# A transformer block on one core: pooling mixer issued before the third head, a serial inverse without raised priority, and four smaller moves

## The chip, the cores and the metric

The kernel runs on one core of a Trainium2 chip. Its engines are TensorE (PE in the profile, with its weight loads as PEld), VectorE (DVE), ScalarE (ACT), GpSimd (POOL) and SyncE (SP, which here only issues transfers). The metric is the device time of one execution in microseconds; the median of three runs is given. The profile comes from one more execution, taken by the hardware profiler.

## The reference

One block of a model on 1024 tokens of width 1024 (f32), cut to what matters here:

```python
h = rms_norm(x, attn_norm)
xa, qkv, z, b, a, c_q, c_kv, k_pe = split(h @ w_in)
y_a = pool_mixer(xa)              # windows 2, 4, 8, 16: (csum - shifted csum)/count - xa, then a 64x64 product per group
y_b = gated_deltanet(qkv, z, b, a)  # conv of 4 taps, silu, 4 heads of 128, chunks: triangular solve, then a serial scan
y_c = mla_attention(c_q, c_kv, k_pe)  # 4 heads, causal softmax
x = x + concat(y_a, y_b, y_c) @ w_out
x = x + square(relu(rms_norm(x) @ w_up)) @ w_down
```

The delta-rule part needs, for each head and chunk, the inverse of a unit triangular matrix and then a scan over chunks in which each step needs the state of the step before.

## The kernel before, in words

**Precision and projections.** Every large product is made of three f32r matmuls on high and low parts (`mm3`, L122): hi·hi, hi·lo, lo·hi. The input projection is cut into 18 column tiles of 128. `proj_tile` (L479) computes one tile in two halves of 512 tokens; a half is 8 x 3 = 24 matmuls of 128x512 into one of four PSUM banks tagged "mm". The tiles run in `tile_order` (L472): 6 to 9 are keys, 14 to 17 gates, 2 to 5 queries, 10 to 13 values, 0 and 1 the input of the pooling mixer. `prefetch` loads the next tile's weights and splits them: ACT casts the high part, and the low part is a subtraction on GpSimd, or on VectorE for the tiles 15, 2 and 10. Two tiles of split weights fit at a time.

**What a half brings.** A query, key or value half is evicted by `conv_silu` (L495): one ACT copy, three scalar-tensor-tensor instructions on VectorE (L502), a tanh on ACT and one product (L510). A value half is then transposed by four TensorE transposes (L697, inside `values`) right after it. A gate half is one ACT and one VectorE instruction (L710). A half of the mixer's input is one ACT copy (L653).

**Side work.** Generators give small steps to be put between halves: after each half `proj_tile` calls `pump(n, m)`, which takes n steps of the queue `side` and m of `slow`. `side` holds first `lanes()` (L576), then `heads(0, 1)`, then `heads(2, 3)`. `lanes()` inverts 128 triangular 32x32 blocks, one per partition, in 31 serial steps of two VectorE instructions (L586, L588), written to memory at its end. In before these stand under `tc.high_priority(offset=3000)`. `heads` runs `levels` (small fp32 products at L751 that build the inverse of 128x128 blocks) and then `chain`, the scan of 8 chunks, for two heads in turn: 76 steps for a pair. 8 steps a half are pumped at the first two gates, SIDE = 10 at queries and values, LATE = 12 at the last gates and mixers.

**Order.** Keys; gates 0, 1; then query and value of heads 0 to 3, with `heads(0, 1)` appended after head 1 and `heads(2, 3)` after head 3; gates 2, 3; first halves of both mixers. Then eight `load_k` (L886 to L893) turn the attention keys; the first mixer's second half stands at the first of them. The attention loop (L1029 on) takes the second mixer's second half in its first group and then `pool` (shifted sums on GpSimd, L612 to L631) and `pool_out`, step by step. `load_v` (L901) splits the attention values on GpSimd. `while slow` pumps `pool(0)` after the key loads.

**After attention.** `out_tile` (L1107) makes 8 x 2 half tiles of x + mixed·w_out. `square` (L1120) squares each on ACT, and GpSimd adds the square into `acc` (L1128); `stats` (L1135) sums over partitions by TensorE from `acc` and the last square; between the second halves the first up-projection weights are split and summed, `s_2` on GpSimd. The MLP follows, in a Strassen-like form.

The instructions are traced in this order, and a planner with a cost model of its own fixes each engine's order at compile time, by order of issue among what it believes ready. On the chip each engine then runs its list in that order.

Of the kernel before, what the change touches and what calls it, by code (L numbers as in the profile page):

```python
# [16 lines left out]
ALU = mybir.AluOpType  # L17
AX = mybir.AxisListType

P = 128  # L20
# [17 lines left out]
YU = 20  # L38
LAG = 2
OFF = 2  # L40
SIDE = 10
LATE = 12
BANKS = {"mm": 4, "sm": 2, "ch": 2, "s2": 2}
WINDOWS = (2, 4, 8, 16)
QK = 96
# [18 lines left out]
def block_kernel(ctx, tc, x, x_t, params, positions, attn_norm, w_tiles, w_g, w_qb, w_kvb, w_out,  # L64
                 w_up, w_down, out, dbg=None):
    nc = tc.nc
# [37 lines left out]
    def MM(tag="mm"):  # L104
        pool, w = (wide[0], 512) if tag == "mm" else (wide[0], 1024) if tag == "s2" else (ps, 512)
        return pool.tile([P, w], F32, tag=tag, name=nm(tag), bufs=BANKS[tag])
# [338 lines left out]
    def load_w(src, shape=(P, KD, P), eng=None):  # L445
        raw = S(shape, "raw", 3)
        nc.sync.dma_start(raw, src)
        hi, lo = S(shape, "w", 4, F32R), S(shape, "w", 4, F32R)
        split(hi, lo, raw, eng)
        return hi, lo  # L450

    side, slow, ahead = [], [], []

    def step(queue, n):
        for _ in range(n):
# [7 lines left out]
    def pump(n, m=0, a=AH):  # L463
        step(slow, m)
        step(ahead, a)
        step(side, n)

    def drain():
        while slow or side or ahead:
            pump(1, 1, 1)  # L470

    tile_order = [6, 7, 8, 9, 14, 15, 2, 10, 3, 11, 4, 12, 5, 13, 16, 17, 0, 1]  # L472
    loaded = {}

    def prefetch(ct):
        if ct not in loaded:
            loaded[ct] = load_w(w_tiles[ct], eng=V if ct in (15, 2, 10) else G)

    def proj_tile(ct, use, n=0, m=1, halves=(0, 1), tag="mm", between=None):  # L479
        prefetch(ct)  # L480
        hi, lo = loaded[ct]
        nxt = tile_order.index(ct) + 1
        for hf in halves:
            if hf == halves[-1] and nxt < len(tile_order):
                prefetch(tile_order[nxt])
            pm = MM(tag)
            for k in range(KD):
                mm3(pm, hi[:, k, :], lo[:, k, :], ht_hi[hf][:, k, :], ht_lo[hf][:, k, :], k == 0, k == KD - 1)
            use(hf, pm)
            pump(n, m)  # L490
            if between and hf == halves[0]:
                between()
# [83 lines left out]
    def lanes():  # L576
        TL = U((P, 32, 32), s="tl")
        TLT = U((P, 32, 32), s="tlt")
        G.memset(TL.rearrange("p a b -> p (a b)"), 0.0)
        G.affine_select(out=TL, in_=TL, compare_op=ALU.not_equal, fill=1.0, base=0, pattern=[[1, 32], [-1, 32]], channel_multiplier=0)  # L580
        tmp = U(s="lt")
        for j in range(31):
            n, m = 31 - j, j + 1
            tv = tmp[:, 512 * (j % 2):512 * (j % 2) + n * m].rearrange("p (a b) -> p a b", a=n)
            with tc.high_priority(offset=3000):
                V.tensor_tensor(tv, L[:, j, j + 1:32].unsqueeze(2).to_broadcast([P, n, m]),  # L586
                                TL[:, j, 0:m].unsqueeze(1).to_broadcast([P, n, m]), op=ALU.mult)
                V.tensor_tensor(TL[:, j + 1:32, 0:m], TL[:, j + 1:32, 0:m], tv, op=ALU.subtract)  # L588
            yield
        with tc.high_priority(offset=3000):  # L590
            V.tensor_copy(TLT, TL.rearrange("p a b -> p b a"))
            nc.sync.dma_start(t_dram[0], TL.rearrange("p a b -> p (a b)"))
            nc.scalar.dma_start(t_dram[1], TLT.rearrange("p a b -> p (a b)"))
        yield

    side.append(lanes())
# [68 lines left out]
    def v4(ap):  # L665
        return ap.rearrange("p (a b) -> p a b", a=4)

    def queries(h):
        qt = QT[h] = U(s="qt")
        proj_tile(2 + h, conv_silu(h, qt), SIDE)  # L670

    def query_key(h):
        qt = QT[h]
# [12 lines left out]
    def values(h):  # L686
        vs = VS[h] = U((P, NC, P), s="vs")
        vt = [None, None]

        def half(hf):  # L690
            vt[hf] = W()
            return vt[hf]

        def use_v(hf):
            pt = MM("sm")
            for j in range(4):
                PE.transpose(pt[:, j * P:(j + 1) * P], vt[hf][:, j * P:(j + 1) * P], ident)  # L697
            for j in range(4):
                c = 4 * hf + j
                A.activation(vs[:, c, :], pt[:, j * P:(j + 1) * P], AF.Copy, scale=sk[:, h, c:c + 1])  # L700

        return 10 + h, conv_silu(8 + h, half, use_v)

    def gate(h):
        zs = ZS[h] = U(s="zs")

        def use_z(hf, pm):
            th = W()
            A.activation(th, pm, AF.Tanh, scale=0.5)
            V.scalar_tensor_tensor(zs[:, hf * 512:(hf + 1) * 512], th, 1.0, pm, op0=ALU.add, op1=ALU.mult)  # L710

        return 14 + h, use_z
# [129 lines left out]
    def heads(*hs):  # L842
        for stage in (levels, chain):
            gens = [stage(h) for h in hs]
            while gens:
                for g in list(gens):
                    try:
                        next(g)
                        yield
                    except StopIteration:  # L850
                        gens.remove(g)
# [1 line left out]
    dn_half = const((P, 1), "dn_half")  # L853
    V.tensor_scalar(dn_half, pv("dn_norm"), 0.5, None, op0=ALU.mult)
    for h in range(2):
        proj_tile(*gate(h), 8, 2)
    for h in range(H):
        queries(h)
        proj_tile(*values(h), SIDE, between=lambda: query_key(h))
        if h % 2:  # L860
            side.append(heads(h - 1, h))
    for h in (2, 3):
        proj_tile(*gate(h), LATE)
    mix = [mixer(i) for i in range(2)]
    for i in range(2):
        proj_tile(*mix[i], LATE, halves=(0,))


    k_hi, k_lo = (S((QK, H, 1024), "H", 4, F32R) for _ in range(2))
# [134 lines left out]
    begin = [[m for m, _ in pairs].index(m) for m in ms_]  # L1004
    turn_at = {max(begin[k] - 1, begin[k - 1]): k for k in range(1, 4)}
    for t in range(NT):
        if t == 0:
            proj_tile(*mix[0], LATE, halves=(1,))
            slow.append(pool(0, XA[0]))
        load_k(t)  # L1010
        pump(2, 1)
        if t == 1:
            load_q(ms_[0])
            turn_q(ms_[0])
            load_q(ms_[1])
    while slow:
        pump(0, 1)
    mid.close()
    wide[0] = mid.enter_context(tc.tile_pool(name="pa", bufs=2, space=PSUM))
    prs = [U(s="pr"), U(s="pr")] + [None] * 4  # L1020

    def mixer_end():
        proj_tile(*mix[1], 0, 0, halves=(1,), tag="sm")
        slow.extend((pool(1, XA[1]), pool_out(0), pool_out(1)))
        yield

    prev = [None] * OFF
    wo_raw = None
    for n in range(len(pairs) + OFF):  # L1029
        if n in turn_at:  # L1030
            turn_q(ms_[turn_at[n]])
            if turn_at[n] < 3:
                load_q(ms_[turn_at[n] + 1])
        if n == 1:
            v_hl = S((P, NT, 2, 4, 64), "H", 4, F32R)
            HB = S((P, 4, 1024), "H", 4)
            prs[2:6] = [HB[:, q, :] for q in range(4)]
            for t in range(NT):
                load_v(t)
        gens, cur = [], None  # L1040
        if n < len(pairs):
            m, hs = pairs[n]
            prp = [prs[(2 * n) % 6], prs[(2 * n + 1) % 6]]
            steps = [1024 // len(hs) if i > 1 else (i + 1) * P for i in (2 * m, 2 * m + 1)]
            gens = [scores(i, hs, prp[i % 2], V if n < 2 else G) for i in (2 * m, 2 * m + 1)]
            if n == 0:
                gens.append(mixer_end())
            cur = (m, hs, prp, steps)
        todo = []
        old = prev.pop(0)  # L1050
        if old:
            pm_, phs, pprp, psteps = old
            todo = [(pm_, hh, j, g, pprp, psteps) for g, hh in enumerate(phs) for j in range(0, 2 * pm_ + 2, 2)]
        while gens or todo:
            if gens:
                try:
                    next(gens[0])
                except StopIteration:
                    gens.pop(0)
                    continue  # L1060
            if todo:
                piece(*todo.pop(0))
                weigh(2)
            step(side, 2)
            if n > 0:
                step(slow, 1)
            if n == len(pairs) and wo_raw is None:
                wo_raw = wo_load(0, "w", 4)
                wo = [S((P, 2, 8, 256), "H", 4, F32R)]
                late = wo_split(wo[0], wo_raw)  # L1070
            if n >= len(pairs):
                next(late, None)
        prev.append(cur)
        while side and n == 1:
            step(side, 1)
# [45 lines left out]
    def square(k, hf, n):  # L1121
        hs = slice(512 * hf, 512 * hf + 512)
        if n == 0:
            return A.activation(acc[:, hs], x2[k][:, hs], AF.Square)
        sq = HM(s="sq")
        ins = A.activation(sq, x2[k][:, hs], AF.Square)
        if n < KD - 1:
            G.tensor_tensor(acc[:, hs], acc[:, hs], sq, op=ALU.add)  # L1128
        else:
            sq_last[0] = sq  # L1130
        return ins
# [416 lines left out]
```

## Time and profile before

| what | value |
|---|---|
| median of 3 runs | 1245.23 us (1244.7 to 1245.61) |
| profiled execution | 1246.01 us |
| its span, first to last instruction | 1243.5 us |
| PE busy | 1173.8 us (94%) |
| DVE busy | 864.1 us (69%) |
| ACT busy | 571.3 us |
| POOL busy | 292.2 us |
| mean granted clock of TensorE | 0.968 |

The span is what the instructions cover; the rest of an execution's time lies around it. A busy PE is not yet a PE at full speed: the granted clock tells which of its two levels (1.2 or 2.4 GHz) it had.

### The profile page before, as it was taken

The numbers are of one execution on the slowest core, as the hardware profiler recorded it, in microseconds if no ns is written. First come the engines' busy times: TensorE is split into PE (matmuls) and PEld (weight loads), VectorE is DVE, ScalarE is ACT, GpSimd is POOL, SyncE is SP. The second block draws the span as 40 slices with busy tenths as digits, with TensorE's granted clock in tenths as the row PEclk, the third lists the DMA queues.
The fourth block names the chain that finished last, engine by engine and source line by source line (L and its number), as shares of the span: only waits on it lengthen the run. The fifth ranks groups of instructions, "written<-read, shape, count | busy, mean of one in ns | idle before, by whom it ended". The sixth has DMA issues, their size and how long they took to land.

```text
span 1243.5 us, 16293 instructions
## 1 busy us (share of the span) xinstructions
PE 1173.8 (94%) x5802; PEld 970.4 (78%) x5802; DVE 864.1 (69%) x1551; ACT 571.3 (46%) x1187; POOL 292.2 (23%) x323
## 2 busy tenths in 40 slices
PE   6999997899999769999799999999999999999998
PEld 5967776788887658788587788888888888888887
DVE  7576659838726758735788776676659897786863
ACT  6554531544534458622346454555554433333330
POOL 0135541011200266422505434243220000000000
PEclk9999999889989779999889999999999999999999
DMA  6102331121120130191314434434469964443202
GB/s 255 65 21 72 132 102 52 60 43 40 30 53 7 62 119 2 62 345 62 108 54 150 176 138 167 154 144 161 148 227 339 375 219 155 152 136 102 94 27 100
DMA packets 85697, 152.60 MB, mean 123 GB/s; under 512 B 25456, under 2 KB 28656, under 8 KB 85616
## 3 DMA queue, kind: packets, MB, share of 16 engines
q1 hardware_dynamic: 76624, 144.23, 32.9%
q10 hardware_dynamic: 8992, 7.34, 1.9%
q8 instruction: 45, 0.74, 0.2%
q14 instruction: 36, 0.29, 0.1%
HBM read 105.41 MB, written 46.14 MB: 122 GB/s over the span
## 4 chain that ended last, share of the span: by engine, by line
PE 74%; DVE 15%; ACT 4%; POOL 4%; issue 2%; DMA 1%; SPq 0%; DVEq 0%; ACTq 0%; POOLq 0%
PE mm L1423 14%; PE mm L1179 13%; PE sm L1179 6%; PE ch L1423 5%; PE sm L1423 5%; PE mm L125 4%; PE mm L123 4%; PE mm L124 4%; PE ch L1179 3%; PE sm L751 2%; DVE t2k L502 2%; DVE H L116 1%; PE ch L125 1%; DVE tl L588 1%; PE ch L123 1%
## 5 line engine op out<-in xcount | busy, mean ns | idle before, releaser
L1423 PE MATMUL mm<-dop,dop 128*128 128x512 f32 x768 | 176.0, 389 | 0.0
L1423 PEld LDWEIGHTS mm<-dop,dop 128*128 128x128 f32 x768 | 144.1, 188 | 29.9
L1179 PE MATMUL mm<-H,wop 128*128 128x512 f32 x576 | 140.2, 396 | 3.8 <-DVE uo L1247 3.8
L1179 PEld LDWEIGHTS mm<-H,wop 128*128 128x128 f32 x576 | 109.4, 191 | 28.2 <-DVE uo L1247 5.1
L115 ACT CAST dop<-wdr 128x1024 fp32r<-128x1024 f32 x48 | 50.4, 1050 | 151.6 <-PE mm L1423 62.9
L123 PE MATMUL mm<-H,w 128*128 128x512 f32 x280 | 115.3, 412 | 2.7 <-DVE zs L710 2.7
L124 PE MATMUL mm<-H,w 128*128 128x512 f32 x280 | 115.0, 411 | 0.0
L125 PE MATMUL mm<-H,w 128*128 128x512 f32 x280 | 114.9, 410 | 0.0
L1179 PE MATMUL sm<-op,wop 128*128 128x512 f32 x384 | 92.2, 389 | 0.0
L116 POOL TENSOR_TENSOR w<-raw,w 128x1024 fp32r<-128x1024 f32 x15 | 36.6, 2438 | 206.2 <-ACT w L115 142.4
L1179 PEld LDWEIGHTS sm<-op,wop 128*128 128x128 f32 x384 | 72.1, 188 | 15.0
L116 DVE TENSOR_TENSOR dop<-wdr,dop 128x1024 fp32r<-128x1024 f32 x48 | 58.6, 1221 | 31.0 <-ACT dop L115 31.0
L1269 ACT ACTIVATE uo<-uo 128x512 f32<-128x512 f32 x48 | 30.3, 631 | 99.4 <-DVE uo L1247 59.2
L1423 PE MATMUL sm<-dop,dop 128*128 128x512 f32 x288 | 67.4, 389 | 0.0
L1423 PE MATMUL ch<-dop,dop 128*128 128x512 f32 x288 | 67.4, 389 | 0.0
L116 DVE TENSOR_TENSOR wop<-s,wop 128x512 fp32r<-128x512 f32 x64 | 47.1, 751 | 26.1 <-ACT wop L115 26.1
L502 DVE SCALAR_TENSOR_TENSOR t2k<-mm,cw,t2k 128x511 f32<-128x511 f32 (+2 forms) x72 | 53.5, 743 | 14.2 <-ACT t2k L499 9.4
L116 DVE TENSOR_TENSOR dop<-H,dop 128x1024 fp32r<-128x1024 f32 x52 | 63.2, 1216 | 0.0
L123 PEld LDWEIGHTS mm<-H,w 128*128 128x128 f32 x280 | 54.0, 193 | 11.6 <-DVE zs L710 3.1
L1423 PEld LDWEIGHTS sm<-dop,dop 128*128 128x128 f32 x288 | 54.1, 188 | 11.2
L1423 PEld LDWEIGHTS ch<-dop,dop 128*128 128x128 f32 x288 | 54.0, 188 | 11.2
L125 PEld LDWEIGHTS mm<-H,w 128*128 128x128 f32 x280 | 54.1, 193 | 8.9
(397 smaller groups left out, 2659.9 us busy)
## 6 DMA issues: line engine op xcount, KB each, us to landing
H<-u_dram SPq DMA_DIRECT2D x52, 512.0 KB, 4.5
upr<-in_w_up_dram SPq DMA_DIRECT2D x38, 512.0 KB, 4.0
u_dram<-t SPq DMA_DIRECT2D x64, 256.0 KB, 2.0
wdr<-in_w_down_dram SPq DMA_DIRECT2D x32, 512.0 KB, 8.1
u_dram<-uo SPq DMA_DIRECT2D x48, 256.0 KB, 2.0
raw<-in_w_tiles_dram SPq DMA_DIRECT2D x18, 512.0 KB, 3.3
wor<-in_w_out_dram SPq DMA_DIRECT2D x10, 512.0 KB, 8.6
x<-in_x_dram SPq DMA_DIRECT2D x8, 512.0 KB, 3.6
```

Of the source, the lines that this page charges most:

```text
L115: A.copy(hi, src)
L116: (eng or V).tensor_tensor(lo, src, f32(hi), op=ALU.subtract)
L123: PE.matmul(o, ah, bh, start=first, stop=False)
L124: PE.matmul(o, ah, bl, start=False, stop=False)
L125: PE.matmul(o, al, bh, start=False, stop=last)
L502: V.scalar_tensor_tensor(acc[:, s:], pm[:, :512 - s], w, acc[:, s:], op0=ALU.mult, op1=ALU.add)
L588: V.tensor_tensor(TL[:, j + 1:32, 0:m], TL[:, j + 1:32, 0:m], tv, op=ALU.subtract)
L751: PE.matmul(pa[:, c, :], lhs[:, c, :], rhs[:, c, :], start=True, stop=True)
L1179: PE.matmul(o, x_, y_, start=(first and j == 0 and q == 0), stop=(j == 3 and q == 2), skip_group_check=True)
L1269: A.activation(o, o, AF.Relu)
L1423: PE.matmul(o, x_[:, cs_], y_, start=(q in (0, 1, 3) and i == 0 and e == 0), stop=(i == GP - 1 and e == 2), skip_group_check=True)
```

## The change

The mixers (tiles 0 and 1) move from the end of the projections to the place between head 1 and head 2 (tiles 4, 12, 5 and 13 come after them), where `heads(0, 1)` starts; `pool(0)` and `pool(1)` are queued right there. The second halves of the gates 2 and 3 take the place that the mixers' halves had beside the key loads. `lanes()` loses its raised priority and is pumped 4 steps a half over gates 0, 1 and head 0. `SIDE` is 7 and `LATE` is gone. The transposes of a value half wait in a list `later` until the next half has been evicted. Weights of tiles 3 and 11 are split on VectorE too. The sums of squares are added on VectorE.

```diff
-SIDE = 10
-LATE = 12
+SIDE = 7
+LANE = 4
...
-    tile_order = [6, 7, 8, 9, 14, 15, 2, 10, 3, 11, 4, 12, 5, 13, 16, 17, 0, 1]
+    tile_order = [6, 7, 8, 9, 14, 15, 2, 10, 3, 11, 0, 1, 4, 12, 5, 13, 16, 17]
...
-            loaded[ct] = load_w(w_tiles[ct], eng=V if ct in (15, 2, 10) else G)
+            loaded[ct] = load_w(w_tiles[ct], eng=V if ct in (15, 2, 10, 3, 11) else G)
...
             pm = MM(tag)
+            due = later[:]
+            del later[:]
             for k in range(KD):
                 mm3(...)
             use(hf, pm)
+            for f in due:
+                f()
             pump(n, m)
...
-            with tc.high_priority(offset=3000):
-                V.tensor_tensor(tv, ...)
-                V.tensor_tensor(TL[:, j + 1:32, 0:m], ...)
+            V.tensor_tensor(tv, ...)
+            V.tensor_tensor(TL[:, j + 1:32, 0:m], ...)
...
         def use_v(hf):
+            later.append(lambda: turn_v(hf))
+
+        def turn_v(hf):
             pt = MM("sm")
...
     for h in range(2):
-        proj_tile(*gate(h), 8, 2)
+        proj_tile(*gate(h), LANE, 2)
     for h in range(H):
-        queries(h)
-        proj_tile(*values(h), SIDE, between=lambda: query_key(h))
-        if h % 2:
-            side.append(heads(h - 1, h))
-    for h in (2, 3):
-        proj_tile(*gate(h), LATE)
-    mix = [mixer(i) for i in range(2)]
-    for i in range(2):
-        proj_tile(*mix[i], LATE, halves=(0,))
+        n = LANE if h < 2 else SIDE
+        queries(h, n)
+        proj_tile(*values(h), n, between=lambda: query_key(h))
+        if h == 1:
+            drain()
+            side.append(heads(0, 1))
+            for i in range(2):
+                proj_tile(*mixer(i), SIDE, 3)
+                slow.append(pool(i, XA[i]))
+    side.append(heads(2, 3))
+    ends = [gate(h) for h in (2, 3)]
+    for z in ends:
+        proj_tile(*z, SIDE, halves=(0,))
...
     for t in range(NT):
-        if t == 0:
-            proj_tile(*mix[0], LATE, halves=(1,))
-            slow.append(pool(0, XA[0]))
         load_k(t)
         pump(2, 1)
         if t == 1:
+            proj_tile(*ends[0], SIDE, halves=(1,))
+        if t == 3:
             load_q(ms_[0])
             turn_q(ms_[0])
             load_q(ms_[1])
+        if t == 5:
+            proj_tile(*ends[1], SIDE, halves=(1,))
...
-    def mixer_end():
-        proj_tile(*mix[1], 0, 0, halves=(1,), tag="sm")
-        slow.extend((pool(1, XA[1]), pool_out(0), pool_out(1)))
-        yield
+    slow.append(pool_out(0))
+    slow.append(pool_out(1))
...
-            if n == 0:
-                gens.append(mixer_end())
...
-            G.tensor_tensor(acc[:, hs], acc[:, hs], sq, op=ALU.add)
+            V.tensor_tensor(acc[:, hs], acc[:, hs], sq, op=ALU.add)
```

## Rows read from the trace of the kernel before

**Rows 1.** The page's head: the span.

```profile
span 1243.5 us, 16293 instructions
```

**Rows 2.** Stretches: time, busy (instructions) of PE, PEld, DVE, ACT, POOL; clock; DMA; GB/s.

```profile
170.00:210.00 40.00, 39.75 (x168) 32.62 (x168) 30.52 (x63) 6.17 (x8) 17.04 (x25) 0.96 0.27 88
210.00:221.00 11.00, 0.23 (x2) 0.02 (x1) 10.05 (x28) 1.23 (x2) 0.00 (x0) 0.73 0.29 120
221.00:256.00 35.00, 33.72 (x178) 28.02 (x179) 26.24 (x60) 20.99 (x66) 8.86 (x8) 0.94 0.22 51
346.00:407.00 61.00, 60.77 (x435) 50.50 (x434) 30.06 (x113) 26.68 (x85) 4.99 (x4) 0.92 0.09 27
407.00:450.00 43.00, 25.90 (x124) 20.80 (x124) 26.57 (x52) 18.15 (x43) 23.20 (x32) 0.73 0.25 84
610.00:618.40 8.40, 0.12 (x2) 0.01 (x1) 5.33 (x5) 3.31 (x6) 8.26 (x6) 0.76 0.16 62
618.40:628.00 9.60, 9.60 (x31) 8.25 (x32) 2.64 (x14) 0.59 (x1) 0.00 (x0) 0.50 0.01 2
```

**Rows 3.** PE's waits over the span: line, waited for, total us, times, longest.

```profile
PE sm L697 <- DVE t2k L510: 11.6, 2, 10.8
PE s L933 <- ACT H L944: 9.1, 3, 6.2
PE ch L1139 <- POOL acc L1128: 8.3, 1, 8.3
PE sm L886 <- DVE H L116: 6.3, 2, 4.7
```

**Rows 4.** VectorE's groups in 184 to 224: count, busy us, mean ns, idle before.

```profile
L588 DVE TENSOR_TENSOR tl<-tl,lt 128x31 f32<-128x31 f32 (+15 forms) x31 | 14.6, 472 | 0.9
L586 DVE TENSOR_TENSOR lt<-lanes,tl 128x31 f32<-128x31 f32 (+15 forms) x31 | 12.7, 409 | 4.0 <-DMA lanes<-a_dram 3.1
L502 DVE SCALAR_TENSOR_TENSOR t2k<-mm,cw,t2k 128x511 f32<-128x511 f32 (+2 forms) x9 | 6.7, 741 | 0.0
```

**Rows 5.** VectorE in time order: start, us, instruction.

```profile
205.48 0.42 DVE L586 TENSOR_TENSOR lt<-lanes,tl 128x252 f32<-128x252 f32 x1
205.94 2.49 DVE L588 TENSOR_TENSOR tl<-tl,lt 128x252 f32<-128x252 f32 x1
220.85 0.74 DVE L502 SCALAR_TENSOR_TENSOR t2k<-mm,cw,t2k 128x511 f32<-128x511 f32 x1
253.52 0.21 DVE L504 SCALAR_TENSOR_TENSOR t2k<-carry,cw,t2k 128x3 f32<-128x3 f32 x1
406.93 1.94 DVE L134 SCALAR_TENSOR_TENSOR sr<-sw,sr 128x4 f32<-128x4 f32 x2
410.91 0.27 DVE L134 SCALAR_TENSOR_TENSOR sr<-sw,sr 128x4 f32<-128x4 f32 x2
445.27 1.56 DVE L629 SCALAR_TENSOR_TENSOR yp<-xs,rw,xa 128x1008 f32<-128x1008 f32 x1 [6.57 <-POOL xs L623]
604.87 3.18 DVE L116 TENSOR_TENSOR wop<-upr,wop 128x512 fp32r<-128x512 f32 x2 [1.21 <-ACT wop L115]
615.91 0.68 DVE L1115 TENSOR_TENSOR x<-mm,x 128x512 f32<-128x512 f32 x1
```

**Rows 6.** GpSimd in time order.

```profile
205.76 2.39 POOL L116 TENSOR_TENSOR w<-raw,w 128x1024 fp32r<-128x1024 f32 x1 [8.53 <-ACT w L115]
406.93 1.92 POOL L623 TENSOR_TENSOR xs<-xa 128x1023 f32<-128x1023 f32 x1 [4.63 <-DVE sw L133]
617.08 1.26 POOL L1128 TENSOR_TENSOR acc<-acc,sq 128x512 f32<-128x512 f32 x1
```

**Rows 7.** ScalarE in time order.

```profile
442.72 1.04 ACT L621 COPY xs<-xs 64x1024 f32<-64x1024 f32 x1 [4.42 <-POOL xs L623]
616.62 0.63 ACT L1126 ACTIVATE sq<-x 128x512 f32<-128x512 f32 x1 [4.00 <-DVE x L1115]
```

**Rows 8.** PE's groups in 346 to 407.

```profile
L124 PE MATMUL mm<-H,w 128*128 128x512 f32 x37 | 16.8, 454 | 0.0
```

More of the change, by code (lines that the diff above doesn't have):

```diff
@@ L450, in load_w @@
         return hi, lo
-    side, slow, ahead = [], [], []
+    side, slow, ahead, later = [], [], [], []
     def step(queue, n):
@@ L584, in lanes @@
             tv = tmp[:, 512 * (j % 2):512 * (j % 2) + n * m].rearrange("p (a b) -> p a b", a=n)
-            with tc.high_priority(offset=3000):
-                V.tensor_tensor(tv, L[:, j, j + 1:32].unsqueeze(2).to_broadcast([P, n, m]),
-                                TL[:, j, 0:m].unsqueeze(1).to_broadcast([P, n, m]), op=ALU.mult)
-                V.tensor_tensor(TL[:, j + 1:32, 0:m], TL[:, j + 1:32, 0:m], tv, op=ALU.subtract)
+            V.tensor_tensor(tv, L[:, j, j + 1:32].unsqueeze(2).to_broadcast([P, n, m]),
+                            TL[:, j, 0:m].unsqueeze(1).to_broadcast([P, n, m]), op=ALU.mult)
+            V.tensor_tensor(TL[:, j + 1:32, 0:m], TL[:, j + 1:32, 0:m], tv, op=ALU.subtract)
             yield
[L590 to L593, printed above, removed]
+        V.tensor_copy(TLT, TL.rearrange("p a b -> p b a"))
+        nc.sync.dma_start(t_dram[0], TL.rearrange("p a b -> p (a b)"))
+        nc.scalar.dma_start(t_dram[1], TLT.rearrange("p a b -> p (a b)"))
         yield
@@ L666, in v4, with queries @@
         return ap.rearrange("p (a b) -> p a b", a=4)
-    def queries(h):
+    def queries(h, n):
         qt = QT[h] = U(s="qt")
-        proj_tile(2 + h, conv_silu(h, qt), SIDE)
+        proj_tile(2 + h, conv_silu(h, qt), n)
     def query_key(h):
```

## The prediction

> **What bounds the kernel now.** I read the page first, then the table of PE's waits, then a table by stage, and last the other engines in time order around each wait. PE is the bound: the span is 1243.5 us [rows 1] and in most stages PE is busy for all of it. So the change can only give back time in which PE stands, or runs at the lower of its two clock levels. Four waits carry nearly all of it [rows 3]: PE's value transposes wait 10.8 us once for VectorE, score matmuls wait 9.1 us for ScalarE, the sums of squares wait 8.3 us for GpSimd, and key transposes wait 6.3 us for VectorE. They lie in three places: 210 to 221, 407 to 450 and 610 to 618 us [rows 2].
>
> In 210 to 221 PE has 0.23 us of work while VectorE is busy for 10.05 of 11 us [rows 2]. VectorE does the 62 lane instructions (27.3 us) and only 9 conv instructions between 184 and 224 [rows 4], so, as I read it, finished halves fill PE's four banks. In 407 to 450 PE is busy 25.90 of 43 us at a clock of 0.73 [rows 2]. Here GpSimd's shifted sums stop two other engines that run their lists in order: VectorE stands 6.57 us before it can finish the second pooling tile [rows 5], ScalarE 4.42 us [rows 7], and the score matmuls wait behind them. In 610 to 618.4 PE has 0.12 us of work [rows 2]; GpSimd's last sum starts at 617.08 [rows 6].
>
> **The change, part by part.** The sum is made against the profiled execution, 1246.01 us, which is its span plus 2.5 us.
>
> *A. Lanes at normal priority, transposes a half later, two weight splits moved.* No lane instruction goes away: 27.3 us stay on VectorE [rows 4]. Its last conv instruction of this stretch, that of head 2's query, starts at 253.52 [rows 5], and the engine is busy for 10.05 of 11 and 26.24 of 35 us on the way [rows 2]; so it is the bound from 184 to 253. What is new is the order: conv instructions no longer queue behind all lanes (the next waits until 220.85 [rows 5]), banks come free one by one, and after head 1 PE finds four mixer halves that cost VectorE nothing. I laid this out half by half: PE 24 x 0.227 = 5.4 us a half (168 matmuls in 39.75 busy us, less 1.6 for a clock of 0.96 [rows 2]), VectorE per half 3 x 0.741 [rows 4] and 0.7 for the product, 4 lane steps of 2 x 0.44 us (the means of rows 4), so 6.4 us against 5.4 over head 0. VectorE still falls behind, and PE still stands at full banks, but in pieces, some filled by transposes. At 240 us PE is then one half further, 5.4 us; with a little of the clock (0.94 over 35 us, of which half is lost: 2.1 us [rows 2]) I take -6. Ends: -13 (10.8 + 2.1, all of it), 0 (the same VectorE work bounds it). The splits of tiles 3 and 11 cost VectorE 2 x 1.2 us (nearest row: 1024 elements at twice the 0.68 of 512 [rows 5]) and leave GpSimd.
>
> That a GpSimd split costs VectorE more than its own time is seen in the trace: a lane instruction that takes 0.42 us takes 2.49 beside a split of 2.39 us that began 0.2 us earlier [rows 5, 6]. So two splits that would fall on lanes cost up to 4.1 us against 2.4, and this edit is about even. The Trainium skill (SBUF — State Buffer, "Who interferes with whom") says that a VectorE instruction with two SBUF inputs and a GpSimd instruction that reads SBUF exclude each other for a whole instruction; the trace agrees, 2.49 against 0.42 us. By that rule the same lock also speaks against part B, see rival 3.
>
> The transposes are as many as before; that they wait one half longer holds a value half in the ring of five 512-wide tiles for 5.4 us more, which the mixers' light evictions cover; without them the next query's eviction would be late by up to one half.
>
> *B. Mixers and pooling beside heads(0, 1).* PE's work is the same: four halves earlier. `heads(0, 1)` is spread over 12 halves at 7 steps instead of 8 at 10. GpSimd's six shifted sums of some 1.9 us and their followers come between weight splits, in a time in which it is mostly idle. On SP the two pooling stores, which wait for VectorE, now stand ahead of later weight loads; those have a whole tile (10.9 us of PE) for load and split, so a store may be some microseconds late before PE notices. The count of 1024-wide tiles reaches the limit of 20 (11 for heads 0 and 1, 8 for their levels, 1 mixer output), so the second mixer's output waits for the levels and head 2's query tile for `pool(0)`. I take 0; ends -3 (bubbles at the norms) and +9 (one wait as long as `pool(1)`'s sums, 4 x 1.9, and its finish, 1.56 [rows 5, 6]).
>
> *C. The stretch after head 3.* What goes: with no pooling here, the 6.2 us and the 2.5 us score waits lose their main cause, and the key waits of 4.7 and 1.5 us lose part of theirs (a pair of norm instructions took 1.94 us beside a shifted sum of 1.92 us, and 0.27 alone [rows 5, 6]). The clock of 0.73 over 43 us means 23 us at the lower level; with PE busy 60% of it, 7 us are lost [rows 2]. That is 17 + 7 = 24 us. What comes: `heads(2, 3)` loses three of seven halves that covered it (37 recorded matmuls of each of three kinds, 111, lie in its 61 us [rows 8, 2]; four halves, 96, remain). Of its 76 steps 14 are pumped at the gates' first halves, 16 at the key loads, 14 at the gates' second halves; 32 go into the attention loop beside the scores. The chain of waits of a step is longer than its own matmuls, so I expect PE bare for some 11 us there, part of it at the lower level, against 24 gained: -13. Ends: -24 and +5 (bare time and clock worth more than what goes).
>
> *D. Squares summed on VectorE.* GpSimd's last sum ends at 618.34 [rows 6], and PE starts 8.28 us after its last output matmul. On VectorE a sum costs about 0.68 us (a 512-wide instruction, [rows 5]); six stand before the end, and each fits into the wait for ScalarE's casts that opens a block (1.21 us [rows 5]), so they add perhaps 1 us. What is late next is VectorE itself: the last tile is evicted at 615.91 and squared at 616.62 to 617.25 [rows 5, 7]. So the wait does not vanish; but the first seven up products, which stood behind the sum, can run in it (9.6 us at clock 0.50 follow the wait [rows 2]), and GpSimd's part goes. I take -5; ends -8 (the wait) and +1.
>
> Sum: -6 + 0 - 13 - 5 = -24, so 1246.0 - 24 = 1222.0 us; against the median of the runs shown, 0.8 us lower than the profiled execution, this is -23 us. All good ends give 1198, all bad ones 1261; neither is likely, as the parts are independent.
>
> **The rivals.**
>
> 1. *VectorE's bound only moves (A is 0, C half).* For it: 27.3 us of lanes stay, and the stretch is VectorE's. Against it: PE is given work that needs no VectorE. 1246 - 0 - 7 - 5 = 1234.
>
> 2. *All three waits go.* A -13, C -20, D -6: 1207. For it: each wait has one engine in order as its cause, and each cause is moved. Against it: the chain's latency.
>
> 3. *Pooling stops heads(0, 1).* Six shifted sums each hold VectorE for about 1.7 us (1.94 against 0.27 [rows 5]), where a serial chain now waits for VectorE: 10 us, 1232. Against it: `heads(0, 1)` has 12 halves as cover. The lock that the Trainium skill states, cited above, is this mechanism.
>
> 4. *Slower: the scan of heads 2 and 3 lies bare.* Place: from the end of head 3's value to the attention loop. PE has some 58 us of work there: the 61 us less 111 matmuls x 0.227, which is 36, and 22 of four halves [rows 2, 8]. If its busy share falls to that of 407 to 450, 0.60 [rows 2], this takes 58 / 0.60 = 97 us, 39 more, of which 11 are in the sum: 1222 + 28 = 1250. It decides from a share of 0.62 down. For it: three halves of cover gone, and the clock falls with the share. Against it: keys and scores are ready to run in the gaps.
>
> **How the numbers follow.** Forecast 0.55, with a range of its own from 1213 to 1231; rival 1 0.13, rival 2 0.12, rival 3 0.10, rival 4 0.10. The range 1206 to 1239 takes in rivals 1 to 3 and leaves out rival 4 and the tails. A difference of 0.2%, 2.5 us, is about what can be told from no change. Faster: forecast, rivals 1 and 2, and most of rival 3, 0.86; within 0.2%: 0.04, from the edge of rivals 3 and 4; slower 0.10.
>
> **What would show it.** A: PE's single wait of 10.8 us for the value transposes is gone, and several of under 5 us stand between 195 and 230; conv instructions lie between lanes. C: no VectorE wait for a shifted sum after the key loads, PE's busy share in the 43 us before pool_out above 0.75. D: PE's wait on `acc` is gone and the next is on the last square or its eviction. B wrong: VectorE or a bank waiting on GpSimd between 260 and 330, or a query eviction late for a tile. The prediction is wrong if PE's waits between head 3 and the scores sum to over 20 us, or if lanes still come in one block.

## The result, and the profile after

The changed kernel takes 1232.26 us (median of 4 runs, 1227.99 to 1232.58), the kernel before, on the same chip, 1245.42 us (1244.7 to 1246.39). The ratio, formed from the means of the runs, is 0.9886, 95% interval 0.9863 to 0.9909: 13 us less by the medians, where 24 were forecast. The profiled execution took 1232.37 us, 13.6 less than that of before. The intervals of the ratios below are 0.25 to 0.5% wide, so a difference of 2 us between two kernels is not told by them.

The page's head gives the span, to be set beside [rows 1].

```profile
span 1230.4 us, 16261 instructions
```

The stretches of [rows 2] at the same times, in the same columns; the last one holds the sums of squares after the output tiles, 618.4 to 628 in [rows 2] and now some 10 us earlier.

```profile
170.00:210.00 40.00, 38.32 (x176) 31.34 (x177) 31.58 (x83) 11.57 (x32) 10.26 (x23) 0.96 0.24 82
210.00:221.00 11.00, 11.00 (x50) 9.09 (x49) 10.83 (x26) 4.32 (x9) 2.41 (x1) 1.00 0.17 53
221.00:256.00 35.00, 31.93 (x203) 25.90 (x202) 14.80 (x35) 14.18 (x41) 8.86 (x8) 0.90 0.34 90
407.00:450.00 43.00, 33.67 (x178) 25.40 (x178) 35.62 (x115) 24.11 (x71) 10.60 (x17) 0.88 0.19 63
608.00:618.00 10.00, 9.73 (x36) 8.10 (x37) 4.14 (x16) 1.65 (x4) 0.00 (x0) 0.68 0.07 28
```

Between 210 and 221 PE is now busy for all 11.00 us, where it was for 0.23. Between 407 and 450 its share rose from 0.60 to 0.78 and its clock from 0.73 to 0.88. The longest of PE's waits in the stages that the change touches (same columns as [rows 3]):

```profile
PE ch L837 <- DVE lv L833: 5.0, 2, 3.1
PE sm L524 <- DVE qt L514: 3.9, 2, 3.1
PE s L942 <- ACT pr L953: 2.7, 1, 2.7
PE ch L818 <- DVE st L816: 2.6, 2, 2.2
PE ch L1144 <- ACT sq L1130: 2.4, 1, 2.4
PE ch L1143 <- DVE acc L1132: 1.3, 1, 1.3
PE sm L702 <- DVE t2k L514: 0.5, 1, 0.5
```

The waits of 10.8, 6.2, 8.3 and 4.7 us of [rows 3] are gone; none here is over 3.1. No VectorE wait for a shifted sum is left behind the key loads. VectorE's groups between 184 and 224, as in [rows 4]:

```profile
L506 DVE SCALAR_TENSOR_TENSOR t2k<-mm,cw,t2k 128x511 f32<-128x511 f32 (+2 forms) x18 | 13.3, 739 | 0.0
L591 DVE TENSOR_TENSOR tl<-tl,lt 128x156 f32<-128x156 f32 (+15 forms) x26 | 13.3, 511 | 0.1
L589 DVE TENSOR_TENSOR lt<-lanes,tl 128x156 f32<-128x156 f32 (+15 forms) x26 | 9.1, 350 | 0.1
```

18 conv instructions (L506) instead of 9 lie in the same 40 us, and five lane steps now come later than 224. At the end of the output tiles PE's list in time order shows what came in place of the wait for GpSimd:

```profile
602.06 0.35 PE L1143 MATMUL ch<-ones,acc 128*128 128x2 f32 x2 [1.33 <-DVE acc L1132]
602.27 0.71 PE L1183 MATMUL mm<-H,wop 128*128 128x512 f32 x2
603.65 2.18 PE L1183 MATMUL mm<-H,wop 128*128 128x512 f32 x5 [0.67 <-DVE wop L116]
608.27 0.58 PE L1144 MATMUL ch<-ones,sq 128*128 128x2 f32 x2 [2.44 <-ACT sq L1130]
```

**Where the 13.6 us came from.** I cut both executions at matching places: the end of the keys, the first level product (L751, now L756) of heads 0 and 1, that of heads 2 and 3, the first output tile, and the end of its sums. One more cut, near 450 us, parts the stretch from heads 2 and 3 to the output tiles in two rows, which the table takes together. Width less PE's busy time is the time that PE stands; 1 less the clock, times the width, is at most what the lower level costs. Before, in the columns of [rows 2]:

```profile
165.00:256.50 91.50, 76.76 (x360) 62.61 (x358) 71.78 (x178) 30.72 (x80) 28.77 (x39) 0.93 0.26 79
256.50:346.00 89.50, 86.38 (x580) 74.19 (x579) 58.47 (x188) 43.93 (x147) 11.37 (x9) 0.92 0.13 31
346.00:450.10 104.10, 86.77 (x558) 71.40 (x558) 56.73 (x164) 44.84 (x127) 28.29 (x35) 0.84 0.16 51
450.10:524.30 74.20, 71.35 (x475) 58.10 (x474) 59.41 (x102) 57.37 (x129) 37.53 (x35) 0.97 0.13 42
524.30:631.30 107.00, 98.72 (x425) 80.91 (x426) 52.59 (x80) 29.73 (x47) 33.24 (x23) 0.94 0.45 158
```

And after:

```profile
165.00:249.30 84.30, 77.52 (x361) 63.06 (x359) 62.17 (x169) 29.66 (x78) 23.97 (x37) 0.94 0.26 84
249.30:364.00 114.70, 109.88 (x669) 91.63 (x668) 69.06 (x201) 53.27 (x157) 30.27 (x27) 0.91 0.14 37
364.00:449.00 85.00, 74.45 (x509) 60.95 (x509) 55.19 (x172) 43.79 (x131) 12.19 (x20) 0.88 0.20 63
449.00:514.00 65.00, 62.29 (x439) 52.51 (x439) 53.02 (x91) 51.02 (x118) 32.38 (x31) 1.00 0.07 23
514.00:618.00 104.00, 98.92 (x427) 80.00 (x428) 59.63 (x93) 30.05 (x47) 16.15 (x11) 0.95 0.45 162
```

| stage | PE stands, before → after | busy at the lower level, before → after | lost (standing + half of that) | change | forecast |
|---|---|---|---|---|---|
| to the first levels (A) | 14.7 → 6.8 | 7.3 → 9.4 | 18.4 → 11.5 | -6.9 | -6 |
| beside heads(0, 1) (B) | 3.1 → 4.8 | 13.7 → 20.5 | 9.9 → 15.1 | +5.1 | 0 |
| heads(2, 3) to the attention's end (C) | 20.2 → 13.3 | 26.7 → 18.7 | 33.5 → 22.6 | -10.9 | -13 |
| output tiles (D) | 8.3 → 5.1 | 9.7 → 7.8 | 13.1 → 9.0 | -4.1 | -5 |
| sum | 46.3 → 29.9 | 57.3 → 56.4 | 74.9 → 58.1 | -16.8 | -24 |

The third column is PE's busy time in the stretches for which the trace has the lower level granted. In the trace of before, matmuls of 128x512 start 0.43 us apart at that level (171.38 and 171.81) and 0.23 us apart at the upper one (174.69 and 174.92), so about half of this time is lost. The last row is the point: PE stands 16.4 us less, but works as long at the lower level as before. The five stages themselves became 13.3 us shorter, not 16.8: PE's busy time in them grew from 419.98 to 423.06 us, although its work is the same, and why it did I can't say.

### The profile page after: what moved, and what is told of

It is laid out like the page before. It is cut to its first block, busy times and chain, and to the rows that moved or that the text cites. A ratio compares the mean times of both kernels' runs of the same rounds, so it can differ in the third digit from the quotient of the medians.

```text
span 1230.4 us, 16261 instructions
## 1 busy us (share of the span) xinstructions
PE 1177.7 (96%) x5802; PEld 972.0 (79%) x5802; DVE 864.9 (70%) x1565; ACT 572.1 (47%) x1187; POOL 264.4 (21%) x309
## 4 chain that ended last, share of the span: by engine, by line
PE 75%; DVE 15%; ACT 4%; issue 3%; POOL 2%; DMA 0%; DVEq 0%; ACTq 0%; POOLq 0%
PE mm L1427 14%; PE mm L1183 12%; PE sm L1183 6%; PE ch L1427 5%; PE sm L1427 5%; PE mm L125 5%; PE mm L123 5%; PE mm L124 5%; PE ch L1183 3%; DVE t2k L506 2%; PE sm L756 2%; PE ch L125 1%; DVE wop L116 1%; PE ch L124 1%; PE ch L123 1%
## 5 line engine op out<-in xcount | busy, mean ns | idle before, releaser
L123 PE MATMUL mm<-H,w 128*128 128x512 f32 x288 | 119.4, 415 | 2.7 <-DVE zs L715 2.7
L125 PE MATMUL mm<-H,w 128*128 128x512 f32 x288 | 118.8, 413 | 0.0
L124 PE MATMUL mm<-H,w 128*128 128x512 f32 x288 | 118.1, 410 | 0.0
L1183 PEld LDWEIGHTS sm<-op,wop 128*128 128x128 f32 x384 | 72.0, 188 | 16.4 <-ACT p L1249 1.5
L1220 POOL TENSOR_TENSOR s<-upr 128x512 f32<-128x512 f32 x16 | 24.3, 1519 | 216.1 <-DVE uo L1209 85.9
L116 POOL TENSOR_TENSOR w<-raw,w 128x1024 fp32r<-128x1024 f32 x13 | 31.9, 2455 | 157.1 <-ACT w L115 153.1
L123 PEld LDWEIGHTS mm<-H,w 128*128 128x128 f32 x288 | 55.8, 194 | 12.1 <-DVE zs L715 3.1
L125 PEld LDWEIGHTS mm<-H,w 128*128 128x128 f32 x288 | 56.3, 195 | 10.2
L124 PEld LDWEIGHTS mm<-H,w 128*128 128x128 f32 x288 | 56.1, 195 | 9.6 <-issue 0.2
```

The costliest lines, as they stand in the source:

```text
L116: (eng or V).tensor_tensor(lo, src, f32(hi), op=ALU.subtract)
L123: PE.matmul(o, ah, bh, start=first, stop=False)
L124: PE.matmul(o, ah, bl, start=False, stop=False)
L125: PE.matmul(o, al, bh, start=False, stop=last)
L1183: PE.matmul(o, x_, y_, start=(first and j == 0 and q == 0), stop=(j == 3 and q == 2), skip_group_check=True)
L1220: G.tensor_tensor(v.s12[:, 0], a21, a22, op=ALU.add)
```

## The experiments

Ratios are to the kernel before, run on the same chip; the changed kernel's is 0.9886. Medians of different experiments can come from different chips, so the ratios are what is compared. Letters of theories hold within one expectation only.

**The lanes' priority put back.**

```diff
+            with tc.high_priority(offset=3000):
                 V.tensor_tensor(tv, ...)
                 V.tensor_tensor(TL[:, j + 1:32, 0:m], ...)
...
+        with tc.high_priority(offset=3000):
             V.tensor_copy(TLT, ...)
...
```

> The changed kernel with the raised priority of the lane steps put back; all else as changed. Theory P (the order of VectorE's work in 184 to 228 is what gave back 7 us of lost PE time ahead of the level products): 1237 to 1240 us, and PE waits some 10 us in one piece for a value or query transpose around 210 to 225. Rival M (VectorE's amount of work is the bound there, and the 7 us come from the mixer halves that PE finds after head 1): 1231 to 1234 us.

Measured: 1234.35 us, ratio 0.9908 (0.9886 to 0.9930), no difference from the changed kernel that can be told. VectorE's groups between 184 and 224:

```profile
L592 DVE TENSOR_TENSOR tl<-tl,lt 128x135 f32<-128x135 f32 (+15 forms) x27 | 13.6, 505 | 0.1
L506 DVE SCALAR_TENSOR_TENSOR t2k<-mm,cw,t2k 128x511 f32<-128x511 f32 (+2 forms) x18 | 13.3, 740 | 0.0
L590 DVE TENSOR_TENSOR lt<-lanes,tl 128x135 f32<-128x135 f32 (+15 forms) x27 | 9.4, 350 | 0.9 <-DMA lanes<-a_dram 0.8
```

Still 18 conv instructions lie there. The rival's time came, not the first theory's: the priority, whose loss I took for one cause of part A, does nothing that can be told once the steps are issued four at a time. That part A was the mixers' place does not follow either (see the third run).

**Squares' sums back on GpSimd.**

```diff
-            V.tensor_tensor(acc[:, hs], acc[:, hs], sq, op=ALU.add)
+            G.tensor_tensor(acc[:, hs], acc[:, hs], sq, op=ALU.add)
```

> The changed kernel with the sums of squares back on GpSimd; all else as changed. Theory P: PE's wait on acc comes back, 7 to 9 us at the end of the output tiles, 4 us more than the two waits of now: 1235 to 1238 us. Rival S (VectorE's last eviction sets the end, the sum does not): 1231 to 1234 us.

Measured: 1236.39 us, ratio 0.9927 (0.9908 to 0.9946). PE's wait is back:

```profile
PE ch L1143 <- POOL acc L1132: 8.5, 1, 8.5
```

The first theory's wait and time came. Part D is worth about 0.4%, 5 us by the ratios; the interval just touches the changed kernel's.

**Mixers, pooling and last gates where they were before, the rest as changed.** The order of tiles, the calls of `mixer`, `pool`, `pool_out` and `gate(2)`, `gate(3)` as in the kernel before, with LATE = 12 and SIDE = 10.

> The changed kernel with mixers, pooling and the last gates where they were before (12 steps a half at the end, 10 at queries and values of heads 2 and 3); lanes, transposes, splits and sums as changed. Theory P (the place of mixers and pooling is worth 5 to 6 us, half of what was forecast): 1236 to 1240 us, with VectorE waiting over 5 us for a shifted sum after the key loads. Rival W (what the move gives back there it loses beside heads 0 and 1, where the lower clock level grew from 13.7 to 20.5 us): 1230 to 1234 us. Rival F (forecast's size, 13 us, hidden by something else): 1243 to 1247 us.

Measured: 1241.88 us, ratio 0.9980 (0.9968 to 0.9993). Of PE's waits:

```profile
PE s L942 <- ACT H L953: 9.1, 3, 6.2
PE ch L838 <- DVE lv L834: 7.2, 4, 4.3
```

and the stretch before the scores:

```profile
402.40:446.00 43.60, 28.54 (x128) 22.19 (x129) 25.21 (x41) 18.20 (x43) 22.80 (x32) 0.68 0.25 83
```

The score waits of [rows 3] are back to the tenth, VectorE again stands 6.6 us for a shifted sum, and PE's share falls to 0.65 at a clock of 0.68. But the first level product still starts at 249, as in the changed kernel, against 257 before. So the mixers' place, with the SIDE and LATE that go with it, is what parts B and C rest on (0.9%, some 12 us by the ratios; the first theory had 5 to 6), and part A does not need it.

**Transposes of a value half at once.**

```diff
-            later.append(lambda: turn_v(hf))
+            turn_v(hf)
```

> The changed kernel with the value transposes right after their half again. Theory P (the planner already puts them later where it sees fit, PE runs far ahead): 1231 to 1234 us. Rival T (the later transposes are what keeps PE from one long wait): 1237 to 1242 us, with a wait of 5 us or more on the value transposes.

Measured: 1233.38 us, ratio 0.9902 (0.9884 to 0.9919): not told from the changed kernel. The wait of value transposes is 3.2 us at its longest instead of 0.5, and the query transposes' 3.1 us goes: the same wait under another name.

**Eight lane steps a half at the two gates, at normal priority.**

```diff
-        proj_tile(*gate(h), LANE, 2)
+        proj_tile(*gate(h), 8, 2)
```

> The changed kernel with 8 lane steps a half at the first two gates, as before the change, so that all 32 are issued ahead of head 0's halves; priority stays normal, all else as changed. VectorE's compiled order shows 6 conv instructions among the lanes here and 18 in the changed kernel, and raising the priority alone changes nothing in it. Theory P (the number of steps pumped per half is what gave back 7 us): 1238 to 1241 us, PE waiting 8 us or more in one piece around 205 to 225. Rival M (PE now has mixer halves to do meanwhile, so the order of the lanes no longer matters): 1231 to 1235 us, and no such wait.

Measured: 1242.54 us, ratio 0.9963 (0.9949 to 0.9977). One long wait is back:

```profile
210.00:217.30 7.30, 0.10 (x2) 0.05 (x1) 6.68 (x21) 0.01 (x1) 0.00 (x0) 0.79 0.26 105
```

PE works 0.10 of 7.30 us while VectorE is busy for 6.68, as between 210 and 221 in [rows 2]; only 9 conv instructions lie between 184 and 224. PE's longest wait for a query transpose is 7.2 us, where the first theory had 8 or more, and the time is above its 1238 to 1241. What carries part A is thus the number of steps issued per half: with eight, all lanes are issued ahead of the convs of head 0, and stand ahead of them in VectorE's list whatever their priority is.

**Splits of tiles 3 and 11 back on GpSimd.**

```diff
-            loaded[ct] = load_w(w_tiles[ct], eng=V if ct in (15, 2, 10, 3, 11) else G)
+            loaded[ct] = load_w(w_tiles[ct], eng=V if ct in (15, 2, 10) else G)
```

> The changed kernel with the weights of tiles 3 and 11 split on GpSimd again; all else as changed. Theory P (even: two splits of 1.2 us on VectorE against two locks of about 2 us): 1231 to 1235 us, and two lane or conv instructions of over 2 us beside the two splits. Rival L (each lock falls on the stretch in which VectorE is the bound and PE's banks are full): 1236 to 1239 us.

Measured: 1239.80 us, ratio 0.9943 (0.9929 to 0.9957), 7 us slower than the changed kernel by the ratios, where the first theory had no difference; the rival was nearer, and the time is above its range too. Of PE's waits:

```profile
PE sm L524 <- DVE qt L514: 7.7, 2, 4.8
```

The wait is 3.8 us longer; the other half of the 7 us I could not tie to a wait. The mechanism of the rival is not shown either. Beside the two splits one lane instruction more is drawn out, from 0.41 to 1.47 us, and the copy that ends the lanes takes 2.0 instead of 1.0 us; VectorE's busy time from 165 to 249.3 us is 62.2 us in both kernels.

**Heads 2 and 3 pushed forward.** Twelve steps a half at the last gates instead of seven, four at each key load instead of two.

```diff
-        proj_tile(*z, SIDE, halves=(0,))
+        proj_tile(*z, 12, halves=(0,))
...
-        pump(2, 1)
+        pump(4, 1)
```

> The changed kernel with 12 side steps a half at the last two gates and 4 at each key load, so that heads 2 and 3 are through before the attention loop; all else as changed. Theory V (beside the scores VectorE is the bound, busy 35.6 of 43 us with the scan in it, and so the scan costs more there than beside the gates): 1225 to 1230 us, PE's waits on the norm and the scan after 400 us gone. Rival K (the scan's own latency is what is bare, wherever it lies): 1232 to 1237 us, with the same waits earlier, among the key loads.

Measured: 1237.06 us, ratio 0.9918 (0.9903 to 0.9934), some 4 us slower than the changed kernel by the ratios, though the intervals overlap a little. The time is just above the rival's range; the first theory's gain did not come. From the first level product of heads 2 and 3 to 440 us:

```profile
361.30:440.00 78.70, 67.43 (x439) 55.49 (x438) 45.55 (x153) 35.20 (x113) 7.32 (x16) 0.80 0.20 59
```

PE stands 11.3 us, about as in the changed kernel (10.6), but at a clock of 0.80 instead of 0.88. Pushing the scan forward did not take its standing away; what lowered the clock is not shown.

**Without the pooling's shifted sums.**

```diff
-        for n, s in enumerate(shifts):
+        for n, s in enumerate(()):
```

> The changed kernel without the shifted sums: the pooling takes the mixer's input as it is, so 8 us of GpSimd sums for the second tile, 4 us for the first and two copies are left out; all else as changed. Theory B (GpSimd's sums beside heads 0 and 1 hold up VectorE, ScalarE or the ring of 1024-wide tiles, and this is the 5 us that the stretch from the level products to head 3 lost): 1225 to 1229 us. Rival Q (they lie beside other work; what the stretch lost is the clock's lower level): 1230 to 1234 us.

Measured: 1229.37 us, ratio 0.9859 (0.9841 to 0.9877); the interval overlaps the changed kernel's, and the time lies between the two theories. The stretch of heads 0 and 1:

```profile
249.00:364.00 115.00, 110.90 (x743) 93.09 (x743) 68.12 (x202) 53.17 (x161) 16.65 (x14) 0.96 0.18 46
```

PE stands 4.1 us in place of 4.8, so without the sums under 1 us of standing goes. What differs more is the clock, 0.96 against 0.91.

**Splits of tiles 0 and 1 on VectorE too.**

```diff
-            loaded[ct] = load_w(w_tiles[ct], eng=V if ct in (15, 2, 10, 3, 11) else G)
+            loaded[ct] = load_w(w_tiles[ct], eng=V if ct in (15, 2, 10, 3, 11, 0, 1) else G)
```

> The splits of the weight tiles 0 and 1 go to VectorE too, beside those of 3 and 11. In the changed kernel two splits on GpSimd of 2.4 us each still lie in the stretch of the lanes (at 212 and 222) and stretch a lane instruction there to 2.5 and 2.35 us. Theory K (the two engines hold each other up while both read and write the core's memory): the two stretched lanes shrink by about 2 us each, VectorE takes on two splits of 1.22 us, the longest wait of query transposes (3.1 us) falls to 1 to 2.5, and the ratio to before is 0.986 to 0.988 (the changed kernel has 0.9886). Rival (the splits on GpSimd hid behind TensorE's work, and VectorE is the engine that is late): the wait rises by the 1.2 to 2.4 us that VectorE takes on, ratio 0.9895 to 0.991.

Measured: 1228.74 us, ratio 0.9858 (0.9834 to 0.9883). VectorE's groups between 184 and 224:

```profile
L506 DVE SCALAR_TENSOR_TENSOR t2k<-mm,cw,t2k 128x511 f32<-128x511 f32 (+2 forms) x18 | 13.4, 743 | 0.0
L591 DVE TENSOR_TENSOR tl<-tl,lt 128x112 f32<-128x112 f32 (+15 forms) x28 | 9.8, 351 | 0.2
L589 DVE TENSOR_TENSOR lt<-lanes,tl 128x112 f32<-128x112 f32 (+15 forms) x28 | 9.8, 348 | 0.1
```

A lane instruction of L591 takes 351 ns in the mean instead of 511, and 28 steps instead of 26 fit in. PE's waits for query transposes fall from 3.9 to 0.9 us. The waits are as the first theory had them; the time by itself does not decide, as the intervals overlap.

**Five lane steps a half.**

```diff
-LANE = 4
+LANE = 5
```

> The lanes advance five steps a half tile instead of four, so that they end about 1.5 halves (some 8 us) sooner; nothing else. Theory R (what carries the gain ahead of the levels is the rate at which the steps are issued, and the waits left there are what one half holds besides its steps): each half gets 0.8 us more of VectorE's work, the longest wait of query transposes goes from 3.1 to about 4 (at eight steps it was 7.2), the first level product comes within 2 us of where it is now, since the queue is emptied at its place in either case; ratio 0.988 to 0.991. Rival (an earlier end of the lanes brings the levels forward by the same time): first level product 3 us or more sooner, ratio below 0.987.

Measured: 1230.83 us, ratio 0.9886 (0.9870 to 0.9903). The first level product comes at 247 instead of 249, and the query transposes wait 0.9 us for VectorE and 1.9 for ScalarE instead of 3.9 for VectorE, where I had expected 4 at once: the size of the step within a half was not what that wait hung on. The first theory's place of the levels and its ratio held. Four or five steps make no difference that can be told; eight do.

**Ten steps of the heads a half.**

```diff
-SIDE = 7
+SIDE = 10
```

> Ten steps of the heads' levels a half tile instead of seven, from the mixers on: heads(0,1) end two to three halves sooner and heads(2,3) crowd the first gate halves. Theory D (a level step's waits lie bare once two steps follow each other with too little of a tile's matmuls between them): the waits of the chain's products on VectorE (L818 and L837, 7.6 us in all in the changed kernel) grow by 3 to 6 us, ratio 0.991 to 0.994. Rival (the waits are covered either way and only the place of the lower-clock time moves): ratio 0.986 to 0.990, and the same waits within 2 us.

Measured: 1232.96 us, ratio 0.9902 (0.9886 to 0.9917). The waits did grow:

```profile
PE ch L837 <- DVE lv L833: 9.8, 3, 4.6
PE ch L818 <- DVE st L816: 0.6, 1, 0.6
```

10.4 us together instead of 7.6, just short of the growth that the first theory had, but no loss of time that can be told: the ratio lies at the rival's edge.

**Splits of tiles 0, 1, 4, 12, 5 and 13 on VectorE.**

```diff
-            loaded[ct] = load_w(w_tiles[ct], eng=V if ct in (15, 2, 10, 3, 11) else G)
+            loaded[ct] = load_w(w_tiles[ct], eng=V if ct in (15, 2, 10, 3, 11, 0, 1, 4, 12, 5, 13) else G)
```

> The splits of the weight tiles 0, 1, 4, 12, 5 and 13 all go to VectorE (the run with 0 and 1 alone had a ratio of 0.9858). Theory K (what held the lanes up holds elsewhere too: while GpSimd splits, VectorE's instruction in flight is drawn out, one of the 128x1 corrections of the convolution to 1.98 us where 0.21 is usual): VectorE trades four stretches of up to 2 us for four splits of 1.22 us, TensorE's gaps from the first level product to the start of heads 2 and 3 (4.8 us in all) fall to 3 to 4.5, and the ratio is 0.983 to 0.986. Rival N (once the lanes are done VectorE is not what TensorE waits for, save in the short chain products, and there a split of 1.22 us ahead of one costs as much as a stretched instruction): gaps of 4.5 to 6.5 us, ratio 0.986 to 0.989.

Measured: 1224.52 us (1219.89 to 1226.68, 5 runs), ratio 0.9827 (0.9808 to 0.9847). This interval lies below that of the changed kernel, so this kernel is the faster one. The first two stages, cut at the same places as above:

```profile
165.00:246.30 81.30, 77.32 (x378) 63.07 (x378) 61.91 (x172) 30.31 (x79) 16.98 (x34) 0.98 0.31 90
246.30:351.00 104.70, 103.23 (x649) 86.70 (x647) 67.49 (x204) 52.30 (x156) 24.00 (x24) 0.93 0.15 39
```

PE stands 4.0 and 1.5 us there instead of 6.8 and 4.8; VectorE, with six splits more, is busy for no longer (61.9 and 67.5 against 62.2 and 69.1 us). Why it isn't can be counted. In these two stages of the changed kernel six instructions of VectorE that ran beside GpSimd took over half a microsecond longer than usual, 9.9 us longer in all; here two did, 2.0 us in all. So 7.9 us of drawn-out time went and 7.3 us of splits came. One thing in the expectation is wrong: the correction of 1.98 us is a 128x2 one, and it lay beside a shifted sum, not beside a split. With 0, 2, 4 and 8 of these splits on VectorE the ratios are 0.9943, 0.9886, 0.9858 and 0.9827; of neighbours only the first two are told apart by their intervals, the ends of the row clearly are.

## Why the prediction came out as it did

**A was right in size, and its cause half wrong.** -6.9 us against -6. The order is as forecast: conv instructions lie between lanes, and PE's standing comes in pieces of at most 3.1 us. But I gave it to the priority, the later transposes and the mixers' cover. Each of these put back alone leaves it: the priority (0.9908), the transposes (0.9902), the mixers (levels still at 249). The rate of issue takes most of it away (0.9963, levels at 255; PE stands 12.9 us in this stage, against 6.8 in the changed kernel and 14.7 before), and the two splits put back take about half of it (10.5 us). My sum had the four steps a half in it, but not as the cause.

**The two splits of A were not about even.** Up to 4.1 us of stretched lanes against 2.4 us of splits was what I had (2 x 1.2; twice the 0.68 of the row is 1.36, and the splits took 1.22 each); the run with both back was 7 us slower, of which 3.7 us is standing in this stage. VectorE's busy time there is the same in both, so adding up the engine's time, as I did, could not show it; why PE stood longer stays open. What [rows 5, 6] show is still there in the changed kernel. VectorE of the changed kernel in time order, around 212:

```profile
211.83 0.41 DVE L589 TENSOR_TENSOR lt<-lanes,tl 128x240 f32<-128x240 f32 x1
212.28 2.48 DVE L591 TENSOR_TENSOR tl<-tl,lt 128x240 f32<-128x240 f32 x1
```

and GpSimd beside it:

```profile
212.09 2.41 POOL L116 TENSOR_TENSOR w<-raw,w 128x1024 fp32r<-128x1024 f32 x1 [31.59 <-ACT w L115]
```

The lane instruction starts 0.19 us after the split and ends 0.26 us after it. In the run with six splits more on VectorE the same instruction took 0.40 us:

```profile
213.83 0.40 DVE L591 TENSOR_TENSOR tl<-tl,lt 128x240 f32<-128x240 f32 x1
```
The rule of the Trainium skill (SBUF — State Buffer, "Who interferes with whom"), that the two engines' shared ports are locked exclusively, agrees with this row and with the two runs that moved more splits to VectorE; 2.48 against 0.40 us is its price here.

**B was wrong.** I took 0; the stage lost 5.1 us more. 1.7 us of it is standing. Both longer waits of the stage come a few instructions after one that GpSimd drew out on VectorE. Before the wait of 1.9 us (L837, at 296.6) a 128x4 instruction took 2.29 us beside a weight split, where 0.16 is usual. Before the wait of 2.2 us (L818, at 319.6) a correction took 1.22 us beside a split, and the next one was drawn out by the pooling's last shifted sum. VectorE of the changed kernel:

```profile
316.30 1.97 DVE L508 SCALAR_TENSOR_TENSOR t2k<-carry,cw,t2k 128x2 f32<-128x2 f32 x1
```

and GpSimd:

```profile
315.91 2.35 POOL L625 TENSOR_TENSOR xs<-xs 64x1016 f32<-64x1016 f32 x1
```

So rival 3, which I gave a chance of 0.10, had named what happens, and B's term left it at nothing. Without the sums the second wait falls to 0.4 us, but one of 1.6 us comes elsewhere. With six splits more on VectorE the same sum runs at 271.8 instead of 315.9, and 3.3 of the 4.8 us of standing go. The other 3.4 us of the 5.1 is the clock: 20.5 us of busy time at the lower level in the profiled execution, against 13.7 before in a stage that was 25 us shorter, as it lacked the mixers' four halves. Nine other kernels whose code in this stage is the same or differs by splits or sums alone (priority, squares' sums, five steps, eight steps, heads 2 and 3 pushed forward, the three split runs and the one without sums) show 10.2 to 20.5 us there. So this part is not a property of the edit that I can show. The changed kernel's own runs differ too, 1227.99 us at a mean clock of 0.979 and 1232.37 at 0.973.

**C was right in kind.** The score waits and the waits for shifted sums went, and the run that put the mixers back brought them back to the tenth. PE stands 6.9 us less, close to the 17 gone less 11 bare that I had; the clock gave 4 us where I had 7. The share from 407 to 450 us, about the 43 us before the end of `pool_out`, is 0.78, above the 0.75 named. Rival 4, the bare scan, did not come: from the first level product of heads 2 and 3 to 449 us PE is busy for 74.45 of 85 us, 0.88.

**D was right.** -4.1 against -5, and the next wait is the last square, 2.44 us, as forecast. The sums on VectorE took 0.69 us each but the last, which met GpSimd's sums for the up-projection. VectorE of the changed kernel in time order:

```profile
600.33 1.58 DVE L1132 TENSOR_TENSOR acc<-acc,sq 128x512 f32<-128x512 f32 x1 [0.76 <-ACT sq L1130]
```

GpSimd beside it:

```profile
600.08 1.29 POOL L1220 TENSOR_TENSOR s<-upr 128x512 f32<-128x512 f32 x1
601.32 1.73 POOL L1230 TENSOR_TENSOR s<-upr,upr 128x512 f32<-128x512 f32 x1
```

**The size as a whole.** The terms of standing in the forecast add up to 16.4 us: 5.4 in A, 0 in B, 17 less 11 in C, 5 in D. The stages show 16.4 us as well, in part by luck, as they came as 8.0, -1.7, 6.9 and 3.2. What was mis-sized is the clock: the forecast had some 7 us come back with the waits in C and under 1 in A. In C 4 us did come back and in D 1, but A and B lost 4.4 again: 57.3 us of busy time at the lower level before, 56.4 after. That, and the 3 us by which PE is busy for longer, is the difference between 24 and 13.6. Rival 1's 1234 lies nearer to the measured time than my 1222, but for a cause that isn't there: A was not nothing. Rival 2 fell with the 10.6 us that PE still stands between the first level product of heads 2 and 3 and 449 us. Rival 3 has its mechanism, with splits beside the sums and a third of its price at most.

The parts do not add up by the runs that put them back. Eight steps a half cost 0.8%, the mixers' old place 0.9% and the sums on GpSimd 0.4%, 2.1% together, where the whole change gave 1.1%. Each was measured with the rest of the change in place; where they overlap no run shows.

**Open.** What sets the place and length of the lower-clock stretches in stages where PE is busy for 95% of the time; why PE stands longer in the run with the two splits back, and where its other 3 us are; and whether the splits of the keys and of the last gates, which are left on GpSimd, would give more on VectorE (not tried).

## What to carry to other kernels

A serial chain that shares an engine with the work that feeds TensorE should be issued a few steps at a time between that work: 4 or 5 steps a half against 8 decided most of part A, and a priority put on top changed nothing that could be told. Before a long two-input instruction is given to an idle GpSimd, ask what VectorE does at that time: six splits moved to the busier VectorE left its busy time where it was and took 0.6% off the kernel. In a forecast, count the standing time that goes, and leave the clock out unless a run shows that it comes back: here the standing came out as added up, and the clock did not.

## What was not expected of the hardware

VectorE's busy time did not rise when it took on six splits of 1.22 us each: 62.2 and 69.1 us in the two stages before that, 61.9 and 67.5 after. The drawn-out instructions on VectorE had cost as much as the splits do, and a 128x2 or 128x4 instruction of some 0.2 us is drawn out by as much as a long one (1.97 and 2.29 us). And two executions of the same program differed by 4.6 us (1227.99 and 1232.58 us), as much as one of the change's parts, with the mean granted clock at 0.979 and 0.975. The stretches at the lower level do not begin at the same places in kernels whose code there is the same: beside heads 0 and 1 at 255.9, 296.9 and 320.8 us in the changed kernel, and at 256.1 us alone in the one with the squares' sums on GpSimd.
